# Two rows of each third unit summed on ScalarE, the first eight rows stored at once, and the last sixteen rows loaded and stored whole

## Chip, cores, metric

One core of a Trainium2 chip. The metric is the device time of one execution in us, median of several; the granted clock is 1.0 in all of them. The experiments were made on two chips; each is compared with the kernel before on its own chip, in the same rounds. The profile's span is 1.3 to 1.5 us shorter than the time, so spans are compared with spans and times with times.

## The reference, cut

```python
x: [16, 1024, 512] float32, gamma: [512], eps = 1e-5
rms = np.sqrt(np.mean(x ** 2, axis=-1, keepdims=True) + eps)
x_norm = x / rms * gamma
return x_norm * (1.0 / (1.0 + np.exp(-x_norm)))
```

Every row of 512 numbers is read once and written once: 33.56 MB each way. Per partition there are 128 rows.

## The kernel before

Rows are worked in 32 units of four rows. ScalarE squares a unit into PSUM (three rows) and sums the fourth by itself, VectorE reduces the three, GpSimd forms the reciprocal root, VectorE multiplies (`norm`), ScalarE applies the swish. Loads are issued by the Sync queue, stores by ScalarE's queue, so there are two DMA queues, q1 and q10 in the profile, called rings here; both are worked by the same 16 DMA engines. `sizes` says how many rows a partition gets in one transfer: a transfer of 16 rows has a run of 32 KB in each partition, and in the trace each such run is one packet (a 16-row transfer shows as 128 packets of 32768 bytes).

```python
sizes = [4, 4, 8] + [16] * 6 + [8, 8]     # loads and stores
ring = 96                                 # rows of buffer in a partition
n_sq = 3
...
def square(k):
    t, at, first = chunks[k]
    if first:
        nc.scalar.wait_ge(ld[t], 16)
    acc = nc.scalar.activation(out=junk[k % 2], in_=xb[:, at + n_sq, :], func=AF.Square,
        scale=inv_d**0.5, accum_out=ms[:, k, n_sq : n_sq + 1])
    ...
    square = nc.scalar.activation(out=sq[k % 2][:, 0:n_sq, :],
        in_=xb[:, at : at + n_sq, :], func=AF.Square, scale=inv_d**0.5)
...
for k in range(K + 3):                    # ScalarE's order
    if k < K:
        square(k)
    while stored < T and ends[stored] <= k - 2:
        store(stored)
        stored += 1
    if 2 <= k < K + 2:
        swish(k - 2)
...
for k in range(K + 1):                    # VectorE's order
    if k < K:
        sums(k)
    ...
    if k >= 1:
        norm(k - 1)
```

## Time and profile before

| | |
|---|---|
| time | 160.23 us (159.91 to 160.41) |
| span of the profiled run | 158.7 us |
| VectorE busy | 138.9 us, 87% |
| ScalarE busy | 125.3 us, 79% |
| moved by DMA | 67.15 MB, mean 423 GB/s |
| last store (2.1 MB) | issued 150.1, landed 158.7 |

The chain's shares add up to 92%, since it ends with the last swish at 150.1 us: the last store, 8.6 us, is not in it. The queue lines (packets, MB, share of the 16 engines' span) and the issue of the last store:

```profile
q1 hardware_dynamic: 1584, 33.56, 49.9%
q10 hardware_dynamic: 1736, 33.57, 49.3%
```
```profile
150.11 0.34 ACTq L189 DMA_DIRECT2D out_dram<-xb  x1
```

The packets fill 99.2% of the span: 157.4 us of work for each DMA engine, and 1.3 us without.

### The profile page before, as it was taken

Reading aid. Unit: us, or ns where it says so; the run is one execution under the profiler, and the core shown is the slowest. Engines: PE = TensorE matmul, PEld = TensorE weight load, DVE = VectorE, ACT = ScalarE, POOL = GpSimd, SP = SyncE. Lnnn points to the kernel's source line nnn. Section 1 sums busy time; section 2 is a strip of 40 time slices with the busy share of each in tenths; the row PEclk is TensorE's granted clock in tenths of the full one; section 3 lists DMA queues with packets and bytes.
Section 4 is the critical chain, followed back from the end, with each engine's and each line's share of the span. In section 5 each row is a group of like instructions: output and inputs, shape, how many; then the busy total and the mean of one; then the engine's idle time right before and its main releaser. Section 6 shows DMA issues by size and latency. Waiting matters only on the chain.

```text
span 158.7 us, 439 instructions
## 1 busy us (share of the span) xinstructions
DVE 138.9 (87%) x162; ACT 125.3 (79%) x129; POOL 65.4 (41%) x71
## 2 busy tenths in 40 slices
DVE  0249999999999999999999999999999999999300
ACT  0935989888888889988888888888998888883600
POOL 2035444444455555544444445555544444445000
DMA  7999999999999999999999999999999999999997
GB/s 235 427 523 405 396 450 419 409 452 407 460 394 413 467 421 452 413 396 479 432 413 429 446 429 413 425 417 458 429 454 396 434 446 438 446 413 438 388 458 301
DMA packets 3324, 67.15 MB, mean 423 GB/s; under 512 B 501, under 2 KB 501, under 8 KB 505
## 3 DMA queue, kind: packets, MB, share of 16 engines
q1 hardware_dynamic: 1584, 33.56, 49.9%
q10 hardware_dynamic: 1736, 33.57, 49.3%
q14 instruction: 4, 0.02, 0.0%
HBM read 33.56 MB, written 33.56 MB: 423 GB/s over the span
## 4 chain that ended last, share of the span: by engine, by line
DVE 85%; DMA 5%; ACT 1%; issue 1%; POOL 0%; POOLq 0%
DVE xb L224 53%; DVE ms L213 32%; DMA gamma<-in_gamma_dram 5%; ACT xb L184 1%; DVE gamma_sb L237 0%; POOL gamma L142 0%; POOL blank L141 0%; POOLq L65 0%
## 5 line engine op out<-in xcount | busy, mean ns | idle before, releaser
L224 DVE SCALAR_TENSOR_TENSOR xb<-xb,rstd,gamma_sb 128x512 f32<-128x512 f32 x128 | 87.4, 748 | 0.0
L184 ACT ACTIVATE xb<-xb 128x2048 f32<-128x2048 f32 x32 | 61.1, 1909 | 17.8 <-DVE xb L224 17.8
L213 DVE TENSOR_REDUCE ms<-sq 128x3 f32<-128x1536 f32 x32 | 56.1, 1754 | 7.0 <-ACT sq L172 7.0
L147 POOL TENSOR_SCALAR aeps<-ms 128x4 f32<-128x4 f32 x32 | 20.6, 644 | 75.2 <-DVE ms L213 75.2
L172 ACT ACTIVATE sq<-xb 128x1536 f32<-128x1536 f32 x32 | 45.9, 1433 | 0.0
L154 POOL TENSOR_TENSOR rstd<-aeps,neg_half 128x4 f32<-128x4 f32 x32 | 44.0, 1376 | 2.7
L165 ACT ACTIVATE junk<-xb 128x512 bf16<-128x512 f32 x32 | 19.7, 615 | 3.4 <-DMA xb<-in_x_dram 3.3
L165 ACT ACTIVATION_READ_ACCUMULATOR junk<-xb 128x1 f32 x32 | 6.0, 186 | 0.0
L199 ACT ACT_TABLE_LOAD x1 | 1.3, 1283 | 3.6 <-issue 3.6
L237 DVE LOAD_MASK_SELECT gamma_sb<-gamma x1 | 0.0, 14 | 2.3 <-DMA gamma<-in_gamma_dram 2.3
L141 POOL MEMSET blank<- 128x16 f32 x1 | 0.1, 111 | 1.5 <-POOLq L65 1.5
L237 DVE STREAM_SHUFFLE gamma_sb<-gamma 128x512 f32<-128x512 f32 x1 | 0.7, 717 | 0.0
L142 POOL MEMSET gamma<- 128x512 f32 x1 | 0.5, 524 | 0.0
L264 POOL MEMSET const-float32-0.0<- 128x1 f32 x1 | 0.1, 98 | 0.2 <-issue 0.2
L264 POOL MEMSET const-bfloat16-1.0<- 128x1 bf16 x1 | 0.1, 102 | 0.0
L264 POOL MEMSET const-uint8-127<- 128x1 uint8 x1 | 0.1, 101 | 0.0
L143 POOL MEMSET neg_half<- 128x4 f32 x1 | 0.1, 101 | 0.0
L264 POOL MEMSET const-float32-1.0<- 128x1 f32 x1 | 0.1, 98 | 0.0
## 6 DMA issues: line engine op xcount, KB each, us to landing
xb<-in_x_dram SPq DMA_DIRECT2D x6, 4096.0 KB, 41.9
out_dram<-xb ACTq DMA_DIRECT2D x6, 4096.0 KB, 31.1
xb<-in_x_dram SPq DMA_DIRECT2D x3, 2048.0 KB, 35.0
out_dram<-xb ACTq DMA_DIRECT2D x3, 2048.0 KB, 10.7
xb<-in_x_dram SPq DMA_DIRECT2D x2, 1024.0 KB, 5.8
out_dram<-xb ACTq DMA_DIRECT2D x2, 1024.0 KB, 20.8
scratch<-blank ACTq DMA_DIRECT2D x1, 8.0 KB, 7.7
gamma<-in_gamma_dram ACTq DMA_DIRECT2D x1, 8.0 KB
```

Of the source, the lines that this page charges most:

```text
L141: nc.gpsimd.memset(blank, 0.0).then_inc(s_blank, 1)
L142: nc.gpsimd.memset(gamma4, 0.0).then_inc(s_zero, 1)
L147: nc.gpsimd.tensor_scalar(out=aeps[:, k, :], in0=ms[:, k, :], scalar1=eps_f, scalar2=None, op0=ALU.add,),
L154: nc.gpsimd.tensor_tensor(out=rstd[:, k, :], in0=aeps[:, k, :], in1=neg_half, op=ALU.pow),
L165: acc = nc.scalar.activation(out=junk[k % 2], in_=xb[:, at + n_sq, :], func=AF.Square, scale=inv_d**0.5, accum_out=ms[:, k, n_sq : n_sq + 1],)
L172: square = nc.scalar.activation(out=sq[k % 2][:, 0:n_sq, :], in_=xb[:, at : at + n_sq, :], func=AF.Square, scale=inv_d**0.5,)
L184: nc.scalar.activation(out=rows, in_=rows, func=AF.Silu), s_norm, k + 1
L199: nc.scalar.preload_act_table_set("silu_and_others")
L213: nc.vector.tensor_reduce(out=ms[:, k, 0:n_sq], in_=sq[k % 2][:, 0:n_sq, :], op=ALU.add, axis=mybir.AxisListType.X,),
L224: ins = nc.vector.scalar_tensor_tensor(out=row, in0=row, scalar=rstd[:, k, j : j + 1], in1=gamma_sb, op0=ALU.mult, op1=ALU.mult,)
L237: nc.vector.stream_shuffle(gamma_sb, gamma4, [0] * 32), s_gld, 16
L264: nc = _bacc.Bacc("TRN2", target_bir_lowering=False, num_devices=1)
```

## The change

Intent: take a third of the reduce off VectorE in every third unit, as ScalarE has 21% idle time, and move the rows in fewer and larger transfers, the last sixteen rows in one load and one store.

```diff
-    sizes = [4, 4, 8] + [16] * 6 + [8, 8]
+    groups = [8, 8] + [16] * 7
+    loads = [(0, 0, 4), (0, 4, 4), (1, 0, 8)] + [(g, 0, 16) for g in range(2, G)]
+    stores = [(0, 0, 8), (1, 0, 8)] + [(g, 0, 16) for g in range(2, G)]
...
-    n_sq = 3
+    def n_sq(k):
+        return 2 if k % 3 == 2 else 3
...
-        acc = nc.scalar.activation(
-            out=junk[k % 2], in_=xb[:, at + n_sq, :], func=AF.Square,
-            scale=inv_d**0.5, accum_out=ms[:, k, n_sq : n_sq + 1],
-        )
+        n = n_sq(k)
+        for j in range(n, cn):
+            acc = nc.scalar.activation(
+                out=junk[j % 2], in_=xb[:, at + j, :], func=AF.Square,
+                scale=inv_d**0.5, accum_out=ms[:, k, j : j + 1],
+            )
...
-            out=sq[k % 2][:, 0:n_sq, :], in_=xb[:, at : at + n_sq, :],
+            out=sq[k % 2][:, 0:n, :], in_=xb[:, at : at + n, :],
```

The entries of `loads` and `stores` are (group, first row, rows). The first store is now of eight rows, where it was two of four; the last load and the last store are of sixteen, where they were two of eight. The rest is bookkeeping: one semaphore for each scratch row of the sums.

## The prediction

> **What bounds the kernel now.** I read the page's slices first, then the chain, then the groups, then transfers one by one.
>
> ```profile
> DVE  0249999999999999999999999999999999999300
> ACT  0935989888888889988888888888998888883600
> ...
> DMA  7999999999999999999999999999999999999997
> DMA packets 3324, 67.15 MB, mean 423 GB/s; under 512 B 501, under 2 KB 501, under 8 KB 505
> ...
> DVE 85%; DMA 5%; ACT 1%; issue 1%; POOL 0%; POOLq 0%
> ```
>
> Two things are full at once. VectorE (DVE) is busy from 13 to 148 us, and the chain that ended last runs over it. But the DMA row is full in every slice, the last included. The chain names whatever ended last; the DMA row says there is no spare time to give back. By windows the rings move 439 GB/s at 140 to 145 us and 430 at 150 to 154; at about 431 GB/s (the mean of a window at 101 to 113 us) 67.15 MB need 155.8 us. They start at 1.9 us (131 GB/s in the second microsecond, 418 after it), which ends them at 157.7 of a 158.7 us span. So VectorE and DMA are balanced within about 1 us, and only a change that also shortens the DMA part can gain more than that.
>
> ```profile
> L224 DVE SCALAR_TENSOR_TENSOR xb<-xb,rstd,gamma_sb 128x512 f32<-128x512 f32 x128 | 87.4, 748 | 0.0
> L184 ACT ACTIVATE xb<-xb 128x2048 f32<-128x2048 f32 x32 | 61.1, 1909 | 17.8 <-DVE xb L224 17.8
> L213 DVE TENSOR_REDUCE ms<-sq 128x3 f32<-128x1536 f32 x32 | 56.1, 1754 | 7.0 <-ACT sq L172 7.0
> ...
> L172 ACT ACTIVATE sq<-xb 128x1536 f32<-128x1536 f32 x32 | 45.9, 1433 | 0.0
> ...
> L165 ACT ACTIVATE junk<-xb 128x512 bf16<-128x512 f32 x32 | 19.7, 615 | 3.4 <-DMA xb<-in_x_dram 3.3
> ```
>
> A unit of four rows costs VectorE 1.67 us (reduce; the chain shows 1.67 where the group has 1754 ns, as neighbours overlap) and 2.65 us (four multiplies): 4.32 us. The timeline of the two engines around 130 us shows how close ScalarE (ACT) is behind:
>
> ```profile
> 132.46 1.75 DVE L213 TENSOR_REDUCE ms<-sq 128x3 f32<-128x1536 f32 x1
> ...
> 136.77 1.76 DVE L213 TENSOR_REDUCE ms<-sq 128x3 f32<-128x1536 f32 x1
> ```
> ```profile
> 132.58 1.91 ACT L184 ACTIVATE xb<-xb 128x2048 f32<-128x2048 f32 x1 [0.46 <-DVE xb L224]
> 134.40 0.61 ACT L165 ACTIVATE junk<-xb 128x512 bf16<-128x512 f32 x1
> ...
> 135.01 1.44 ACT L172 ACTIVATE sq<-xb 128x1536 f32<-128x1536 f32 x1
> ```
>
> A norm ends at 132.54, its swish and then the next squares follow, and those end at 136.45; the reduce that needs them starts at 136.77. The loop of norm, swish, squares has only 0.3 us of slack per unit.
>
> **What the Trainium skill says.** "DMA: Bandwidth & Descriptors", section "Queues, rings and completion order": each DMA engine takes turns between the rings with work, packet by packet. The trace agrees if a packet is one partition's run. Loads (q1) and stores (q10) both of 32 KB runs, 62 to 79 us, then loads of 16 KB against stores of 32 KB, 101 to 113 us:
>
> ```profile
> q1 hardware_dynamic: 118, 3.77, 51.3%
> q10 hardware_dynamic: 115, 3.67, 50.2%
> ```
> ```profile
> q10 hardware_dynamic: 103, 3.38, 65.1%
> q1 hardware_dynamic: 112, 1.80, 35.0%
> ```
>
> Half and half, then two to one: the run size sets the share. "VectorE: DVE Perf Modes", "Mode 1× (REGULAR) — the baseline", and the page's 0.96 GHz clock: one result a cycle, so 512 elements fewer are 0.53 us. The 1754 ns for 1536 elements (1600 plus 154) agree. "ScalarE: Activation LUTs", "What ACT_TABLE_LOAD costs": 0.833 ns an element and about 93 ns of overlap; 1433 minus 615 ns over 1024 elements is 0.80, close.
>
> **The change, part by part.**
>
> (1) In 10 of 32 units the reduce has two rows: minus 0.53 us each, 5.3 us on VectorE. ScalarE gains a sum (0.61 us from start to next start) and its squares lose 0.43 (estimate, 512 times 0.833 ns): plus 0.19 a time, beside VectorE's work. But the unit after a short reduce comes due in 4.32 - 0.53 = 3.79 us while the ScalarE loop needs (136.45 - 132.54) + 0.08 overlap + 0.03 handover = 4.02. So VectorE waits some 0.24 us there, and of 0.53 only 0.29 stays: 2.9 us in all.
>
> (2) Ledger of the rings, at 0.431 MB/us: 4.19 MB (16 rows) takes 9.7 us alone, 19.5 against stores of the same run; 14.6 against a 16 KB store, 12.2 against an 8 KB one. Test it on the kernel before. The first three loads (4.19 MB) end at 11.6. Store 0, issued at 18.0, landed 16.5 us later at 34.5; less 12.2 it took its first turn at 22.3 (a lump of 4.3 for queued loads and landing). Then stores land at 46.7, 61.3, 80.8 (measured 47.5, 62.0, 81.3). Loads got 4.6 MB by 22.3 and 12.6 by 61.3; the 3.8 MB left of the five 16-row loads at half rate end at 78.8; the next 16 rows at 98.3; the two 8-row loads, at one third of the rate, at 112.9 and 127.5. Measured landings are 82.4, 101.8, 116.4, 130.9: always 3.5 later[...], so I carry 3.5 over.
>
> After: store 0 has eight rows and comes at 22.5, first turn 26.8; it and store 1 (16 KB) end at 41.4 and 56.0, store 2 at 75.5, all earlier than its load needs. Loads: 6.5 MB by 26.8, 14.9 by 56.0, the rest of the five at 84.0; group 7 at 103.5; group 8, whole and at half rate, at 123.0, landing 126.5.
>
> (3) Who waits for it: unit 28, its first. Before, its sum of squares started at 125.77 (by the cadence: unit 30's at 134.40 less two units of 4.32) with its 8-row load there since 116.4, and the rest needed only at 134.4. After, eight short units by then (a ninth, unit 2, is lost: unit 4 asks for a load that landed only at 22.3) make ScalarE ready at about 123.4; it waits 3.1 us for the whole group. The 2.3 us won are spent and some more.
>
> (4) The tail, walked with the durations above from 126.55: squares 28 end 128.6, reduce 28 and norm 27 end 133.0, squares 29 (two sums) 132.6, reduce 29 and norm 28 end 136.8, squares 30 136.9, reduce 30 and norm 29 end 141.3, squares 31 140.7, reduce 31 and the last two norms end 148.3, swish 31 ends 150.2. Before, the last swish ended at 150.1: nothing gained on the compute side.
>
> (5) The last store is 4.19 MB rather than 2.1, issued at 150.2. All other bytes are through at 157.7 - 9.7 = 148.0, so the rings run dry, where before the half-group issued at 143.2 kept them busy to the last store. From issue to first packet 1.0 to 1.3 us (the first load, on empty rings, started its bytes 1.0 after its issue), so 151.4; plus 9.7 is 161.1; plus 0.5 to 1.0 for landing: span about 161.7. Time is span plus 1.3 to 1.5 (160.02 against 158.7 in the profiled run, 160.23 the median): 163.0, that is 1.7% slower.
>
> **The rivals.**
> A, VectorE is the bound: minus 5.3 or (with the ScalarE loop) 2.9 us, 155 to 157. For it: the chain is 85% VectorE. Against: the DMA row, full to the end; the same bytes have to move.
> B, the last group lands before ScalarE asks (by 123.4). Then the last swish ends at about 147.3, the store comes as the rings empty, and nothing is lost or won: about 160 to 161. For it: the ledger is good to perhaps 1 us, and the 2.9 us would be real. Against: the landing would have to be 3 us early.
> C, the whole group is worse than I think: a load that lands at 127.5, or more time from issue to first byte, each one for one: 164 to 165.
> D, small waits for loads from unit 20 on as ScalarE runs ahead. Group 7 lands at 107.0 by the ledger, about when unit 24 asks. These are swallowed by the wait at unit 28.
>
> **Range and chances.** Steps 3 and 5 pass errors on one for one; the landing carries 0.7 us, the tail 0.5. I say 163.0, 161.3 to 164.2. The 2% line is 163.43, 0.4 above my value: slower over 2% 0.33, within 0.65, faster 0.02.
>
> **What would show it.** A group of 22 reduces of 1754 ns and 10 of about 1220; a short VectorE wait for squares in each third unit; one ScalarE wait of about 3 us for a load near 123 to 126.5; the last store issued near 150.2 and landing 11.5 us later; DMA slices below 9 tenths around 149 to 151. If there is no ScalarE wait at unit 28, B holds; if DMA stays full to the end and the time falls, I am wrong about DMA.

## The result, and the profile after

162.68 us (162.48 to 162.92) against 160.2 in the same rounds: ratio 1.0157, 95% interval 1.0135 to 1.0178: slower by 1.6%, clear of noise, and the same by the 2% line that the prediction uses. Ratios here and below are the mean time of one kernel's fast runs over that of the other's of the same rounds, so not quite the ratio of the medians quoted.

The slices and the chain of the changed kernel:

```profile
DVE  0249999999999999999999999999999499997000
ACT  0835999998998998998998998999896689847200
...
DMA  7999998999999999999999999999999999996696
...
DMA packets 2891, 67.15 MB, mean 417 GB/s; under 512 B 452, under 2 KB 452, under 8 KB 456
...
DMA 54%; DVE 23%; ACT 13%; issue 1%; POOL 0%; ACTq 0%; POOLq 0%
```

VectorE has a hole (the 4) at about 126 us, and two DMA slices, from 145 to 153 us, fall to 6 tenths, where the kernel before had 9. The chain now runs over DMA for 54% of the span: over a store and the last load (49%) and the load of gamma (5%). VectorE's busy time fell by 4.4 us (134.5, from 138.9), and the span still grew by 2.5. The queue lines say where that went:

```profile
q1 hardware_dynamic: 1440, 33.56, 49.2%
q10 hardware_dynamic: 1448, 33.57, 48.4%
```

97.6% of 161.2 us are 157.3 us of work for each DMA engine, as before (157.4), and 3.9 us without work, where it was 1.3. The engines move the same bytes in the same time, and all the added span is time in which they have nothing to move.

The groups by shape (columns as on the page) show the two parts of the sum change, of 10 units each:

```profile
L227 DVE TENSOR_REDUCE ms<-sq 128x3 f32<-128x1536 f32 x22 | 38.6, 1753 | 11.2 <-ACT sq L185 9.9
...
L227 DVE TENSOR_REDUCE ms<-sq 128x2 f32<-128x1024 f32 x10 | 12.1, 1215 | 0.0
L185 ACT ACTIVATE sq<-xb 128x1024 f32<-128x1024 f32 x10 | 10.0, 1005 | 0.0
```

The timeline of ScalarE (start, us, then what, and in brackets the idle time before it) at unit 28 and at the end:

```profile
126.27 0.63 ACT L176 ACTIVATE junk<-xb 128x512 bf16<-128x512 f32 x1 [2.80 <-DMA xb<-in_x_dram]
...
148.09 1.91 ACT L197 ACTIVATE xb<-xb 128x2048 f32<-128x2048 f32 x1 [0.74 <-DVE xb L238]
150.03 0.34 ACTq L202 DMA_DIRECT2D out_dram<-xb  x1
```

ScalarE waits 2.80 us for the last load, and the last store is issued at 150.03, where the kernel before issued its last, half as large, at 150.11. The windows (busy of VectorE, ScalarE and GpSimd, clock, DMA share, GB/s; a packet counts where it starts) from 148 to 151 us, first of the kernel before, then of the changed one:

```profile
148.00:149.00 1.00, 0.14 (x1) 0.83 (x1) 0.00 (x0) 1.00 0.73 311
149.00:150.00 1.00, 0.00 (x0) 1.00 (x1) 0.00 (x0) 1.00 1.22 524
150.00:151.00 1.00, 0.00 (x0) 0.08 (x1) 0.00 (x0) 1.00 1.03 442
```
```profile
148.00:149.00 1.00, 0.06 (x1) 0.91 (x1) 0.00 (x0) 1.00 0.01 0
149.00:150.00 1.00, 0.00 (x0) 1.00 (x1) 0.00 (x0) 1.00 0.00 0
150.00:150.50 0.50, 0.00 (x0) 0.01 (x1) 0.00 (x0) 1.00 0.00 0
150.50:150.80 0.30, 0.00 (x0) 0.00 (x0) 0.00 (x0) 1.00 0.00 0
```

In the changed kernel no packet of data starts from 148 to 150.8 us. In the kernel before the stream goes on. By the packet records the last packet before the hole ends at 148.90 and the next begins at 150.87: all 16 engines stand still for 2.0 us, and some of them had run out before that. The store before the last landed at 149.3 (issued 134.7, 14.6 us to landing), the last one took 11.1 us alone.

### The profile page after: what moved, and what is told of

It reads as the page before. It is cut to its first block, busy times and chain, and to the rows that moved or that the text cites. A ratio compares the mean times of both kernels' runs of the same rounds, so it can differ in the third digit from the quotient of the medians.

```text
span 161.2 us, 455 instructions
## 1 busy us (share of the span) xinstructions
DVE 134.5 (83%) x162; ACT 126.5 (78%) x149; POOL 65.4 (41%) x71
## 4 chain that ended last, share of the span: by engine, by line
DMA 54%; DVE 23%; ACT 13%; issue 1%; POOL 0%; ACTq 0%; POOLq 0%
DMA xb<-in_x_dram 31%; DMA out_dram<-xb 18%; DVE xb L238 15%; DVE ms L227 8%; ACT xb L197 7%; DMA gamma<-in_gamma_dram 5%; ACT sq L185 4%; ACT junk L176 2%; DVE gamma_sb L251 0%; POOL gamma L149 0%; POOL blank L148 0%; ACTq L173 0%; POOLq L67 0%
## 5 line engine op out<-in xcount | busy, mean ns | idle before, releaser
L227 DVE TENSOR_REDUCE ms<-sq 128x3 f32<-128x1536 f32 (+1 forms) x32 | 50.7, 1585 | 11.2 <-ACT sq L185 9.9
L185 ACT ACTIVATE sq<-xb 128x1536 f32<-128x1536 f32 (+1 forms) x32 | 41.6, 1299 | 0.0
L176 ACT ACTIVATE junk<-xb 128x512 bf16<-128x512 f32 x42 | 25.8, 615 | 6.7 <-DMA xb<-in_x_dram 6.6
L176 ACT ACTIVATION_READ_ACCUMULATOR junk<-xb 128x1 f32 x42 | 7.8, 186 | 0.0
```

The lines of the kernel that those rows point to most:

```text
L176: acc = nc.scalar.activation(out=junk[j % 2], in_=xb[:, at + j, :], func=AF.Square, scale=inv_d**0.5, accum_out=ms[:, k, j : j + 1],)
L185: square = nc.scalar.activation(out=sq[k % 2][:, 0:n, :], in_=xb[:, at : at + n, :], func=AF.Square, scale=inv_d**0.5,)
L227: nc.vector.tensor_reduce(out=ms[:, k, 0 : n_sq(k)], in_=sq[k % 2][:, 0 : n_sq(k), :], op=ALU.add, axis=mybir.AxisListType.X,),
```

## The experiments

Theory T: the DMA rings are the floor; time is lost only when they run dry, and they do because the last store is whole and is issued after everything else has gone out. Rivals: V, VectorE's time sets the end; S, the additional sums make ScalarE the bound; L, the late whole load is what costs, by itself.

**Only the two-row sums, on the kernel before.**

```diff
 # kernel before; groups, loads and stores unchanged
-    n_sq = 3
+    def n_sq(k): return 2 if k % 3 == 2 else 3
 # and the loop over the sums of the change
```

> The kernel before with only the two-row sums of the change; groups, loads and stores as before. Theory T (DMA is the floor): last swish 2.5 to 2.9 us earlier, near 147.4, and the time the same, 160.2 (159.8 to 160.5), as the last bytes still end at 158. Rival V (VectorE sets the time): 157.3, 1.8% faster. Rival S (ScalarE's extra sums become the bound): 160.5 or more, with the last swish no earlier.

Measured: 160.03 us, ratio to the kernel before 0.9989 (0.9973 to 1.0005). The last store is issued at 147.35, 2.76 us earlier than before, and lands at the same time: 11.3 us after its issue, for 2.1 MB, because it queues. Its slices:

```profile
DVE  0249999999999999999999999999999999996000
...
DMA  6999999999999999999999999999999999999997
```

VectorE stops earlier, DMA doesn't. V (157.3) falls, and so does S (no earlier last swish).

**VectorE nearly halved, on the kernel before** (three of four rows are not normalized). Its output is wrong, which doesn't matter for the time.

```diff
-        for j in range(cn):
+        for j in range(1):
             row = xb[:, at + j, :]
```

> The kernel before with only one of the four multiplies of each unit (wrong result on purpose): VectorE loses about 2.0 us of 4.32 a unit, 63 us in all, and all transfers stay. Theory T: the rings stay full and the time is 159.5 to 160.3, the same. Rival V (VectorE is the bound): ScalarE becomes the bound at 3.86 us a unit, so about 14 us less, near 146.

Measured: 160.28 us, ratio 1.0012 (0.9999 to 1.0025).

```profile
DVE 78.0 (49%) x66; ACT 123.2 (78%) x129; POOL 54.6 (34%) x71
...
DMA  7999989999899999999999999999999999999997
```

VectorE is busy for 78.0 us rather than 138.9 and the time stays. ScalarE waits 17.0 us for loads instead. This is the plainest of the runs: the engine over which 85% of the chain went could lose 61 us without a change in the time.

**Only the grouping, three rows in every unit.**

```diff
-        return 2 if k % 3 == 2 else 3
+        return 3
```

> The changed kernel with three rows of squares in every unit, as before the change, so only the grouping is left. Theory T: ScalarE asks for unit 28 near 125.8 and the load lands near 126.2, a wait of under 1 us; the last store is issued at 150 to 150.8, rings dry before it; time 162.3 to 163.2, the same as the changed kernel within 0.5: the two-row sums bought nothing there. Rival V (VectorE time counts): 2.9 us slower than the changed kernel, about 165.5. Rival S (the extra sums on ScalarE cost): faster than the changed kernel, near 160.

Measured: 162.92 us, ratio to the kernel before 1.0161 (1.0140 to 1.0182): the changed kernel's loss, without its sums. ScalarE's wait at unit 28 shrinks to 0.64 us, since it comes later, and the last store is issued at 151.0. So within the new grouping the sums bought nothing: what ScalarE gains on the way it waits off at the last load.

**The last store in two halves.**

```diff
-stores = [(0, 0, 8), (1, 0, 8)] + [(g, 0, 16) for g in range(2, G)]
+stores = [(0, 0, 8), (1, 0, 8)] + [(g, 0, 16) for g in range(2, G - 1)]
+         + [(G - 1, 0, 8), (G - 1, 8, 8)]
```

> The changed kernel with its last store in two halves of eight rows; the last load stays whole. Theory T (the rings are full except where they run dry before the last store): the ScalarE wait at unit 28 stays at about 2.8 us and the last store is still issued near 150.0, but the half stored before it keeps the rings busy; span 158.8, time 160.2 (159.8 to 160.7), like the kernel before. Rival L (the late whole load is what costs): time stays near 162.5, as the last swish does not move. Rival V (VectorE and ScalarE set the end): 162.5 less at most the 2 us of a shorter last transfer, about 160.5 too, so V is not told from T here but by the two-row and three-row kernels.

Measured: 160.62 us, ratio 1.0022 (1.0004 to 1.0040). The wait is still there, and the last store is issued no earlier (150.78 in the slowest of its six runs, whose first loads already land some 0.4 us later); yet six sevenths of the loss are gone (1.57% to 0.22%). The wait and the windows:

```profile
127.01 0.63 ACT L176 ACTIVATE junk<-xb 128x512 bf16<-128x512 f32 x1 [2.96 <-DMA xb<-in_x_dram]
```
```profile
148.00:149.00 1.00, 0.81 (x2) 0.26 (x2) 0.00 (x0) 1.00 1.00 426
149.00:150.00 1.00, 0.00 (x0) 1.00 (x1) 0.00 (x0) 1.00 1.03 442
150.00:151.00 1.00, 0.00 (x0) 0.75 (x1) 0.00 (x0) 1.00 0.88 377
```

The half store issued at 143.8 fills the hole. L falls in its simple form: the late load alone costs nothing that can be told from 0.2%.

**The last load in two halves.**

```diff
-loads = [(0, 0, 4), (0, 4, 4), (1, 0, 8)] + [(g, 0, 16) for g in range(2, G)]
+loads = [(0, 0, 4), (0, 4, 4), (1, 0, 8)] + [(g, 0, 16) for g in range(2, G - 1)]
+        + [(G - 1, 0, 8), (G - 1, 8, 8)]
```

> The changed kernel with its last load in two halves of eight rows, the last store whole. Theory T: runs of 16 KB against stores of 32 KB get a third of the rate, not half, so by the ledger the first half lands near 121 (no wait at unit 28) and the second near 135.5, where ScalarE asks for unit 30 at about 131.6: the wait moves from unit 28 to unit 30 and is 3 to 4 us; last store issued 150.5 to 151, time 163 (162.4 to 163.8). Rival L (the whole load is what costs): no wait, last swish 2.5 us earlier, time about 160.5.

Measured: 164.51 us, ratio 1.0260 (1.0241 to 1.0279): slower still, a little above the range I gave. The halves landed at 121.7 and 136.5; the second is 10.3 us later than the whole load of the changed kernel. Rings from 110 to 120 us, and the wait at unit 30:

```profile
q10 hardware_dynamic: 99, 2.72, 63.1%
q1 hardware_dynamic: 97, 1.56, 36.3%
```
```profile
136.56 0.63 ACT L176 ACTIVATE junk<-xb 128x512 bf16<-128x512 f32 x1 [3.93 <-DMA xb<-in_x_dram]
```

Cutting a load in two, to have the first half sooner, halved its runs and with them its turn against stores of 32 KB runs. The last store went out at 152.0 and landed 11.1 us later again. The expected wait (3 to 4 us) came. What was short is the landing, 1.0 us after the 135.5 expected; from it to the last store are 15.5 us, as walked (15.0 to 15.5).

**The first store in two of four rows, on the changed kernel.**

```diff
-stores = [(0, 0, 8), (1, 0, 8)] + ...
+stores = [(0, 0, 4), (0, 4, 4), (1, 0, 8)] + ...
```

> The changed kernel with its first store in two of four rows (8 KB runs, the first issued near 18.0 as in the kernel before), all else as changed, the last load and the last store whole. Theory T: small early stores take less of the rings from the loads, so by the ledger the last load lands near 121.3 to 123, about when ScalarE asks (123.4); wait under 0.8 us, last store issued near 147.3, just before the rings empty (148.5); time 160.3 (159.9 to 161.2). If the first stores' size does not set the landing, 162.5 as the changed kernel.

Measured: 160.44 us, ratio 1.0025 (1.0012 to 1.0038). A change to a store at 18 us moved the landing of the last load from 126.2 to 120.4 us, and ScalarE does not wait at unit 28. The last store, still whole, is issued at 147.48, before the store ahead of it lands (149.4), and lands at 159.1. So a whole last store costs little (0.25% in all here) if it comes before the rings are empty. ScalarE at unit 28, with no idle time in brackets, and the last store:

```profile
123.20 0.61 ACT L176 ACTIVATE junk<-xb 128x512 bf16<-128x512 f32 x1
...
147.48 0.34 ACTq L202 DMA_DIRECT2D out_dram<-xb  x1
```

**The last sixteen rows whole, on the kernel before.**

```diff
-    sizes = [4, 4, 8] + [16] * 6 + [8, 8]
+    sizes = [4, 4, 8] + [16] * 7
```

> The kernel before with its last two groups of eight made one of sixteen, loaded and stored whole; three rows of squares everywhere, first stores of four rows. Theory T: the last load lands near 121 to 123, before ScalarE asks at 125.8, no wait; the last store is issued at 150.1 as in the kernel before, but whole and after the rings ran dry near 148.6; time 162.4 (162.0 to 162.9). That is the cost of the whole last store alone. Rival L (the late load is what costs): 160.2.

Measured: 162.87 us, ratio 1.0170 (1.0157 to 1.0183). The load lands at 121.0 and ScalarE starts unit 28 at 126.1 without a wait; the last store is issued at 150.5 and lands 11.1 us later. The loss of the changed kernel is here in full with no late load and no additional sums:

```profile
126.13 0.61 ACT L165 ACTIVATE junk<-xb 128x512 bf16<-128x512 f32 x1
...
150.47 0.34 ACTq L189 DMA_DIRECT2D out_dram<-xb  x1
```

**Both repairs, the candidate.**

```diff
-stores = [(0, 0, 8), (1, 0, 8)] + [(g, 0, 16) for g in range(2, G)]
+stores = [(0, 0, 4), (0, 4, 4), (1, 0, 8)] + [(g, 0, 16) for g in range(2, G - 1)]
+         + [(G - 1, 0, 8), (G - 1, 8, 8)]
```

> The changed kernel with its first store in 4 and 4 rows and its last store in 8 and 8: the candidate. Theory T: nothing waits and the rings never run dry, yet no gain over the kernel before: 160.0 (159.6 to 160.4), as 67.15 MB at 431 GB/s and the start are the floor; the last store queues some 3 us longer than in the kernel before. Rival V: 157.5.

Measured: 160.46 us (one run of six at 161.59), ratio 1.0038 (1.0016 to 1.0060). That is just above the range expected, and it doesn't beat the kernel before. Nor does it beat the kernel with the last store alone in halves (1.0022), whose load is late: nothing is left of L. No version beats the kernel before: the runs point to a floor of about 160, set by 157 us of packets in each DMA engine (156.9 to 157.6 in all ten profiles, by their queue lines). No run moved fewer bytes to see the floor itself go down.

Four kernels issue a whole last store onto empty rings, and their ends differ as the issues do (all times in us):

| kernel | last store issued | span | issue to end of span |
|---|---|---|---|
| changed | 150.03 | 161.2 | 11.2 |
| last whole, on before | 150.47 | 161.6 | 11.1 |
| grouping only | 151.01 | 162.1 | 11.1 |
| last load in halves | 152.00 | 163.2 | 11.2 |

## Why the prediction was right

It was right in the time (163.0, measured 162.68), in the range and in the class it favoured; and the path was right too, from the ledger to the hole at the end. By its steps:

1. *The sums are worth 2.9 us and not 5.3.* The last store of the kernel with the sums alone comes 2.76 us earlier. A reduce of two rows takes 0.54 us less (1753 less 1215 ns; 0.53 was estimated from the page "VectorE: DVE Perf Modes"). The squares of two rows take 0.43 us less (1433 less 1005 ns), as estimated from 0.833 ns an element; the 0.80 that the prediction found compares two kinds of instruction, and like with like the trace gives 0.836. The wait of VectorE after a short unit shows in the changed kernel's VectorE timeline:

```profile
93.21 2.73 DVE L238 SCALAR_TENSOR_TENSOR xb<-xb,rstd,gamma_sb 128x512 f32<-128x512 f32 x4
96.08 1.76 DVE L227 TENSOR_REDUCE ms<-sq 128x3 f32<-128x1536 f32 x1
```

   With 2.65 us for the multiplies the reduce could start at 95.86; it starts 0.22 later (0.24 predicted). VectorE's waits list doesn't show it: its 9.9 us are three waits, 7.1 at the start, 2.29 at unit 28 and 0.45 at unit 24.

2. *The ledger of the rings.* Predicted ends of the first three stores 41.4, 56.0 and 75.5; measured landings 41.9, 57.4 and 76.7. Last load 126.5; measured 126.2. The 3.5 us that it adds to every load are fitted to the kernel before, and no run shows their cause. (Its sums hold, with one slip of wording: the 12.6 MB are what the loads got between 22.3 and 61.3 us, 17.2 MB with the 4.6 before.) Its rule, that the turn goes by runs, was tested afresh by cutting the last load (121 and 135.5 expected, 121.7 and 136.5 measured) and by cutting the first store (121.3 to 123 expected, 120.4 measured, and 121.4 in the candidate).

3. *The wait at unit 28.* 3.1 us predicted, 2.80 measured.

4. *The tail.* Last store predicted at 150.2, measured at 150.03.

5. *The dry rings.* This term was the worst sized. I had the rings dry from 148.0 to 151.4, 3.4 us; they were dry from 148.90 to 150.87, 2.0 us. The store's first packet began 0.84 us after its issue (0.84 or 0.85 in all four kernels of the table), where I said 1.0 to 1.3 and used 1.2. Landing was 161.13 against 161.7: 0.17 us from the earlier issue, 0.4 from here. The profiled run is the fastest of the four (162.48); against the median the error is 0.3.

Rival A (VectorE is the bound) is refuted by the two kernels that take VectorE time away. The reading that the DMA row is full "in every slice, the last included" was too strong, as the first and the last show 7 tenths; nothing was built on those two. Rival B (the load lands early enough) did not happen, and the kernel with the small first stores shows what it would have been: 160.44. Rival C (a landing at 127.5, or a longer way to the first byte) did not happen either: 126.2, and 0.84 us. Rival D, small waits ahead of unit 28, came as one of 0.19 us at unit 24, and was swallowed.

What the prediction only touched, in rival B, and the runs show: the loss needs two things together, a whole last store and an issue of it after the rings have emptied. At 147.48, before the store ahead had ended, it cost next to nothing; from 150.03 on it cost 1.6% and more; no run lies between. With the load late and the store in halves 0.22% is left of it; with the store whole but the load early and the sums in, 0.25%. The late load is one way to be late; three rows of squares in every unit are another (kernel before, last sixteen whole: 1.7% with no late load). With the sums the whole store would have come early enough, had the first store not been doubled to eight rows. What stays open is the 0.2 to 0.4% by which the repaired versions lie above the kernel before; no run here tells their causes apart (the 0.38% of the candidate is 0.20% without its one run at 161.59).

## What to carry to other kernels

Before taking work off the engine that the chain names, divide the bytes by the rate that the DMA row shows and compare with the span: if they are within a per cent or two (here 155.8 of 158.7 us), suspect that the engine's time is already hidden; here 61 us less of it changed nothing, and the changes that made a difference were those that opened a hole in the transfers. Multiply the queues' shares by the span: if the product stays (157.4 and 157.3 us here) and the span grows, the engines waited. Look for the hole at the end: here the last store had to be small, or be issued while the one before it was still moving. And where two rings share the engines, as here, the run length of a transfer acted as its priority (runs of 16 KB against 32 KB got 35% of the engines' time), so the size of an early store could decide when the last load lands.

## What the Trainium skill lacked or had wrong

- "DMA: Bandwidth & Descriptors", Specifications, gives about 358 GB/s as the HBM limit of one core, which is too low as it stands for one core alone: this program moved 423 GB/s over the whole span of the kernel before, and 431 from 101 to 113 us. The page's fabric ceiling of 435 GB/s is what these runs come near. (Further down, the same page has 425 GB/s measured for a core alone, and calls 358 the share when both cores of a pair stream; the table doesn't say so.)
- The same page, "Queues, rings and completion order", gives the turn by packet, but not what follows for the shares: runs of 32 KB against 32 KB shared the engines 51.3% to 50.2%, 16 KB loads against 32 KB stores 35.0% to 65.1%. Nor does it say how far this reaches: the last load landed 4.8 to 5.8 us later when the first store, some 100 us before, was one of eight rows and not two of four (126.2 against 120.4 and 121.4).
- The same page gives about 0.6 us to the first byte for a transfer issued from ScalarE's or Sync's queue, and doesn't say from where it counts. The last store, on empty rings, started its first packet 0.84 us after the start of its issue, 0.50 after the end of the issuing instruction (0.34 us); the first load of the kernel 1.00 and 0.63.
- "ScalarE: Activation LUTs", "What ACT_TABLE_LOAD costs": 186 ns plus 0.833 ns an element, with no word on the destination, gives 1039 ns for 1024 elements and 1466 for 1536; squares written to PSUM took 1005 and 1433, some 33 ns less. For 512 elements written to SBUF it gives 613, and 615 was measured.
